# The first group's keys for four token tiles abreast, begun with half of w_ada's columns, with the first gate unit beside them

## The chip, the cores and the metric

The kernel runs on one core of one Trainium2 chip. The metric is device time in microseconds (us). Before the change the median of three runs is 1931.95 us (1931.21 to 1932.6). The engines are TensorE (PE; its weight loads are a row of their own, PEld), VectorE (DVE), ScalarE (ACT), GpSimd (POOL) and SyncE (SP), which issues every DMA here. Each engine takes its instructions strictly in the order in which they stand in its own program.

## The reference

One encoder layer is applied to two request groups (prompt and sample, each 1024 tokens by 1024 channels) with the same weights. A vector c per group gives shift, scale and gate; the input is RMS-normed and modulated; one wide projection feeds two attention branches and their gates:

```python
mod = jnp.einsum('bd,de->be', jax.nn.silu(c), w_ada) + b_ada
shift, scale, gate = jnp.split(mod, 3, axis=-1)
h = rms_norm(x, norm_g) * (1.0 + scale[:, None, :]) + shift[:, None, :]
proj = jnp.einsum('bsd,de->bse', h, w_in)
qa, ka, va, za, qb, kb, vb, zb, ga, gb = jnp.split(proj, [o1, o2, o3, o4, o5, o6, o7, o8, o9], axis=-1)
qa = rms_norm(qa.reshape(B, S, HQ_A, HEAD_DIM), qn_a)      # ka the same way, then both rotated
...
oa = gqa_attention(qa, ka, va) * jax.nn.silu(za)
ob = rms_norm(diff_attention(qb, kb, vb, lam), subln_g) * (1.0 - lam_init) * jax.nn.silu(zb)
merged = jax.nn.sigmoid(ga) * (oa @ w_proj_a) + jax.nn.sigmoid(gb) * (ob @ w_proj_b)
out = x + gate * (merged @ w_out)
```

(The last four lines are shortened here; the shapes are left out.)

## The kernel before

All matmuls of the projection work on pairs: a float32 operand is split into a rounded part ("hi", made by ACT with a Copy) and the rest ("lo", a subtraction), and a product is three matmuls, hi*hi, hi*lo and lo*hi. Weights are split by `split_w` (L192 on ACT, L194 on DVE or POOL), the modulated input h by `modulated`.

**The start of the first group** is `start`. SP issues, in order, two tiles of w_ada (1 MB each), small vectors, the first half of the transposed input (tokens 0 to 511, 2 MB), the other six tiles of w_ada that give shift and scale, the weights of keys and values (`C_KA`, 256 columns, 1 MB), and the other half of the input. w_ada comes in eight tiles: numbers 0 and 1 give the shift of channels 0 to 511, 2 and 3 their scale, 4 and 5 the shift of channels 512 to 1023, 6 and 7 their scale. For each pair, `ada` makes eight thin matmuls (L324), then `ada_end` copies the row (L342 on DVE), lays it as columns (L336, four matmuls of two columns) and adds the bias (L348, L352), which fills `modc`. Meanwhile ACT squares the input, DVE adds the squares (L278 to L283), PE sums them over the partitions (L291), POOL takes the power -1/2 (L301) and `spread` (L308) lays the result over the partitions. `x` is then multiplied by it (L394, six on DVE and two on POOL), scaled and shifted (L358 on ACT, L360 on DVE), and split (L363 on ACT, L364 on DVE). All this is done for eight chunks of 128 channels.

**The head of the first group** is `head`. Two streams are woven on PE: keys and values (`kva_gen`) for eight token tiles and then the first half of the queries (`qa_gen`), through `proj_tt` (L539: per token tile 8 chunks x 3 matmuls of 128x256), and the gate units (`z_gen`, L709: each unit 8 x 3 matmuls of 128x512). After each token tile `front` normalises and rotates on DVE (lines 554 to 582, with one power on POOL, L560), and `back` transposes on PE (L593) and splits (L595 on ACT, L596 on DVE); `LAG = 2` lets a token tile's `back` come two tiles later. Between the first two tiles and the rest, `start_late` normalises and modulates tokens 512 to 1023 (L412, L415 to L417). Then attention begins: scores (L743, L744), the maximum (L745, DVE), the exponential (L746, ACT), while further gate units and queries fill PE.

**The rest**: attention of branch A and B with the remaining projections woven in, the branch projections, the output projection; `ht_gen` prepares the second group's h beside the first group's output projection; then the second group goes through the same stages.

**What sets the order.** The kernel writes its instructions in the order of these generators; a scheduler then sets each engine's order from a model of its own, within the data dependences, the number of buffers in each pool, and the extra edges that `behind` adds. PSUM has two 1024-wide tiles `s`, three 512-wide `f` and one `a`. `gbank` takes an `s` tile for two of every five requests while attention is not running (`alone`).

## Time and profile before

| | us |
|---|---|
| median of three runs (range) | 1931.95 (1931.21 to 1932.6) |
| the profiled execution, its own time | 1934.43 |
| its span in the profile | 1932.7 |
| busy: PE, PEld, DVE, ACT, POOL | 1863.8, 1562.7, 1161.5, 760.0, 674.2 |
| mean granted TensorE clock | 0.985 |

The span begins with the first instruction, and the profiled execution lasts 1.7 us longer than it. In the rows of a timeline stand the start in us, the length from the first start to the last end, the engine, the line, the operation, the tiles (result<-operands, buffer numbers left out), the shape and the count; in brackets the engine's idle time ahead of it and what ended it. A row of a table by stretches gives, for each engine, the busy us and the number of instructions, then the granted clock (PEclk, 1.00 is full), the share of DMA time and GB/s. Matmuls overlap in the pipeline, so the rate is read from starts: two rows that begin 24 matmuls apart.

### The profile page before, as it was taken

The numbers are of one execution on the slowest core, as the hardware profiler recorded it, in microseconds if no ns is written. First come the engines' busy times: TensorE is split into PE (matmuls) and PEld (weight loads), VectorE is DVE, ScalarE is ACT, GpSimd is POOL, SyncE is SP. The second block draws the span as 40 slices with busy tenths as digits, with TensorE's granted clock in tenths as the row PEclk, the third lists the DMA queues.
The fourth block names the chain that finished last, engine by engine and source line by source line (L and its number), as shares of the span: only waits on it lengthen the run. The fifth ranks groups of instructions, "written<-read, shape, count | busy, mean of one in ns | idle before, by whom it ended". The sixth has DMA issues, their size and how long they took to land. (4 is left out here: it accounts for less than half of the span.)

```text
span 1932.7 us, 29441 instructions
## 1 busy us (share of the span) xinstructions
PE 1863.8 (96%) x10434; PEld 1562.7 (81%) x10434; DVE 1161.5 (60%) x1709; ACT 760.0 (39%) x1548; POOL 674.2 (35%) x912
## 2 busy tenths in 40 slices
PE   6989999999999998999999999999999899999999
PEld 3778878888888996788888777888888798877887
DVE  5787663444667366757467777445357736666731
ACT  4444442444445344323233455234445524442210
POOL 2233421433456254121222434024456616322110
PEclk8999999999999999999999999999999999999999
DMA  8136674546243355875631567564525423587531
GB/s 316 54 87 172 182 200 133 156 128 201 81 137 100 98 169 156 268 259 179 209 104 50 166 183 198 157 180 132 163 78 143 111 79 90 157 251 248 170 103 55
DMA packets 268883, 295.03 MB, mean 153 GB/s; under 512 B 35136, under 2 KB 217536, under 8 KB 268736
## 3 DMA queue, kind: packets, MB, share of 16 engines
q1 hardware_dynamic: 268736, 293.15, 51.0%
q8 instruction: 83, 1.36, 0.3%
q14 instruction: 64, 0.52, 0.1%
HBM read 133.59 MB, written 42.01 MB: 91 GB/s over the span
## 5 line engine op out<-in xcount | busy, mean ns | idle before, releaser
L709 PE MATMUL f<-u,w 128*128 128x512 f32 x2256 | 588.4, 398 | 1.3 <-ACT w L192 0.9
L539 PE MATMUL f<-w,u 128*128 128x256 f32 x3456 | 484.0, 286 | 1.9 <-DVE ev L719 0.9
L709 PEld LDWEIGHTS f<-u,w 128*128 128x128 f32 x2256 | 415.2, 190 | 85.2 <-issue 2.7
L539 PEld LDWEIGHTS f<-w,u 128*128 128x128 f32 x3456 | 456.8, 192 | 24.2 <-issue 2.7
L745 DVE TENSOR_REDUCE m<-s 128x1 f32<-128x1024 f32 x256 | 309.9, 1218 | 208.3 <-PE s L744 205.9
L746 ACT ACTIVATE p<-s,m 128x1024 f32<-128x1024 f32 x256 | 285.2, 1115 | 287.4 <-DVE m L745 219.2
L194 POOL TENSOR_TENSOR w<-st,w 128x512 fp32r<-128x512 f32 x168 | 223.0, 1345 | 455.9 <-ACT w L192 415.4
L787 DVE STREAM_TRANSPOSE p<-p 128x1024 f32<-128x1024 f32 x192 | 237.0, 1240 | 69.0 <-ACT p L746 59.3
L560 POOL TENSOR_TENSOR rs<-ss,nhalf 128x4 f32<-128x4 f32 (+1 forms) x112 | 109.1, 975 | 361.7 <-DVE ss L559 317.8
L744 PE MATMUL s<-u,sw 128*128 128x512 f32 x512 | 204.8, 400 | 0.0
L192 ACT ACTIVATE w<-st 128x512 fp32r<-128x512 f32 x196 | 115.1, 626 | 147.1 <-DMA st<-in_w_in_dram 92.2
L946 PE MATMUL f<-u,w 128*128 128x512 f32 x552 | 137.4, 398 | 3.9 <-DVE u L957 3.2
L819 PE MATMUL a<-q,u 128*128 128x256 f32 x512 | 132.8, 394 | 8.0 <-DMA q<-p 5.5
L946 PEld LDWEIGHTS f<-u,w 128*128 128x128 f32 x552 | 103.7, 190 | 27.4 <-DVE u L957 4.8
L819 PEld LDWEIGHTS a<-q,u 128*128 128x128 f32 x512 | 98.6, 198 | 24.9 <-issue 5.9
L802 PE MATMUL a<-q,u 128*64 128x256 f32 x1024 | 117.6, 382 | 1.0 <-DMA q<-p 1.0
L743 PE MATMUL s<-u 128*128 128x512 f32 x256 | 108.0, 422 | 10.2 <-ACT p L746 8.9
L596 DVE TENSOR_TENSOR u<-f,u 64x256 fp32r<-64x256 f32 (+1 forms) x196 | 80.6, 411 | 58.1 <-ACT u L595 53.1
L743 PE MATMUL s<-u,u 128*128 128x512 f32 x256 | 104.9, 410 | 8.4 <-DVE ev L719 4.3
L744 PEld LDWEIGHTS s<-u,sw 128*128 128x128 f32 x512 | 97.4, 190 | 17.5 <-issue 0.8
L977 PE MATMUL f<-u,w 128*128 128x512 f32 x456 | 105.6, 389 | 0.0
L786 DVE SCALAR_TENSOR_TENSOR p<-p,r,p 128x1024 f32<-128x1024 f32 x64 | 87.2, 1362 | 28.8 <-POOL r L772 24.2
(168 smaller groups left out, 1939.7 us busy)
## 6 DMA issues: line engine op xcount, KB each, us to landing
q<-p SPq DMA_DIRECT2D x768, 128.0 KB, 2.6
st<-in_w_in_dram SPq DMA_DIRECT2D x132, 256.0 KB, 3.1
zd<-ev SPq DMA_DIRECT2D x96, 256.0 KB, 2.6
sw<-u SPq DMA_DIRECT2D x256, 64.0 KB, 2.0
p<-zd SPq DMA_DIRECT2D x64, 256.0 KB, 4.1
u<-in_w_ada_dram SPq DMA_DIRECT2D x8, 1024.0 KB, 11.4
od<-oo SPq DMA_DIRECT2D x64, 128.0 KB, 2.4
st<-in_w_in_dram SPq DMA_DIRECT2D x64, 128.0 KB, 2.8
```

The costliest lines, as they stand in the source:

```text
L192: nc.scalar.activation(wh, st, AF.Copy)
L194: e.tensor_tensor(out=wl, in0=st, in1=wh.bitcast(F32), op=ALU.subtract)
L539: ins = nc.tensor.matmul(ps, lt[c][:, sl], w[:, c, wi, :], start=(k == 0), stop=(k == 23))
L709: ins = nc.tensor.matmul(ps, w[:, c, wi, e * P : (e + 1) * P], rt[c], start=(k == 0), stop=(k == 23),)
L743: nc.tensor.matmul(s[:, sl], q, k[:, sl], start=True, stop=False)
L744: nc.tensor.matmul(s[:, sl], sw, k[:, sl], start=False, stop=True)
L745: nc.vector.tensor_reduce(out=m, in_=s, axis=AX.X, op=ALU.max, negate=True)
L746: nc.scalar.activation(pt.rearrange("p (j c a) -> p j c a", j=4, c=8), s.rearrange("p (c a j) -> p j c a", c=8, j=4), AF.Exp, bias=m, accu ...
L787: nc.vector.transpose(pt, pt)
L802: lambda k=k, m=m: nc.tensor.matmul(acc[(LO, HI)[m]], u["v"][:, k], pT[m][:, k], start=(k == 0), stop=(k == 7))
L819: nc.tensor.matmul(acc, u["v"][:, k], pT[:, k], start=(k == 0), stop=(k == 7))
L946: nc.tensor.matmul(ps, w[:, c, wi, d * P : (d + 1) * P], o[:, oi, :], start=(k == 0), stop=(k == 11))
```

## The change

1. **Transfers and columns.** SP now issues two tiles of w_ada, the first half of x, w_ada 2 and 3, then the first half (512 channels) of the weights of keys and values, w_ada 4 and 5, the first half of the first gate unit's weights (`C_ZA`), w_ada 6 and 7, the second half of the keys' weights, the second half of x, and the second half of the gate's weights; the tables of the rotation come behind all these.
2. **Keys abreast.** `abreast` works chunk by chunk on four token tiles at once, in four accumulators that lie in the two `s` tiles. Chunks 0 to 3 need only w_ada 0 to 3, and are issued before the matmuls of w_ada 6 and 7; chunks 4 to 7 follow. Two gate units of 24 matmuls (256 columns of the gate in two times 128, tokens 0 to 511) are begun with chunks 0 to 3 as well, in an `a` and an `f` tile, and finished later. Then the second four token tiles are done abreast, with the third gate unit between, and the fourth behind them.
3. **A shorter modulation.** `modulate` replaces `modulated`, the tail of `start_late` and the body of `ht_gen`: per chunk DVE multiplies by scale and 1/rms in one instruction, ACT adds the shift and rounds (hi), DVE makes lo from x, shift and hi. The separate multiplication by 1/rms (L394), and in `ht_gen` the addition on POOL, are gone.
4. **Smaller edits.** The lo part of weights is always made on POOL (before: on DVE for every other piece while `alone`). `ada_end` lays its columns in the accumulator itself. `gbank` takes `s` tiles only from the middle of the first head on. The key's transposes of the first group use the `a` tile until then. The exponential of lambda is put behind a later instruction of ACT.

Line numbers below are those of the changed kernel: L336 is `ada`, L348 the laying of columns, L385, L391 and L378 the three instructions of `modulate` (DVE, ACT, DVE), L408 `abreast`, L780 `z_part`, L655 and L659/L660 the keys' and queries' transposes and splits, L602 `proj_tt`.

```diff
--- before.py
+++ after.py
...
+    wide = [False]
 
     def gbank():
         turn[0] += 1
-        if alone[0] and turn[0] % 5 in (0, 2):
+        if wide[0] and alone[0] and turn[0] % 5 in (0, 2):
             return sbank()[:, :512]
...
-        e = nc.vector if alone[0] and q % 2 else nc.gpsimd
+        e = nc.gpsimd
...
+    def split_early(w, half, sts):
+        for i, st in enumerate(sts):
+            split_w(w, half * 2 + i, st)
...
+    def load_early(pieces):
+
+        room = halves2(ptile())
+        sts = [r.rearrange("p (c n) -> p c n", c=2) for r in room]
+        for st, srcs in zip(sts, pieces):
+            load_piece(st, srcs)
+        return sts
...
-        row = halves2(ptile())[0]
+        row = rtile()
         nc.vector.tensor_copy(row, acc)
-        ps = gbank()[:, :8].rearrange("p (c g) -> p c g", g=2)
+        ps = acc[:, :8].rearrange("p (c g) -> p c g", g=2)
...
-    def modulated(ht, hf, xT, cs):
...
+    def modulate(ht, hf, xs, rsb, g=0):
+
+        acts = []
+
+        def low(c, x):
+            hi, lo = (part[c] for part in ht[hf])
+            return nc.vector.scalar_tensor_tensor(
+                out=lo, in0=x, scalar=modc[:, 0, c, g : g + 1], in1=hi.bitcast(F32), op0=ALU.add, op1=ALU.subtract
+            )
+
+        prev, ins = None, None
+        for c, x in xs + [(None, None)]:
+            if x is not None:
+                new = nc.vector.scalar_tensor_tensor(
+                    out=x, in0=x, scalar=modc[:, 1, c, g : g + 1], in1=rsb, op0=ALU.mult, op1=ALU.mult
+                )
+                if ins is not None:
+                    behind(new, ins)
+                ins = new
+                acts.append(nc.scalar.activation(ht[hf][0][c], x, AF.Identity, bias=modc[:, 0, c, g : g + 1]))
+            if prev:
+                new = low(*prev)
+                behind(new, ins)
+                ins = new
+            prev = c, x
+        return ins, acts
...
+    def four():
+        return [s[:, n * 512 : n * 512 + 256] for s in (sbank(), sbank()) for n in range(2)]
...
+    def abreast(ht, w, hf, ps, cs):
+
+        for c in cs:
+            for i in range(4):
+                sl = slice(i * P, (i + 1) * P)
+                for n, (part, wi) in enumerate(((0, 0), (0, 1), (1, 0))):
+                    latest[0] = nc.tensor.matmul(
+                        ps[i], ht[hf][part][c][:, sl], w[:, c, wi, :],
+                        start=(c == n == 0), stop=(c == NCH - 1 and n == 2),
+                    )
...
+    def start(ht, kva, zs):
+        front, back = kva
         nc.scalar.activation(cT[:, : NCH * 2], cT[:, : NCH * 2], AF.Silu)
         wts = [load_ada(n) for n in range(2)]
         dma(bcol, t["b_col"])
         dma(gcol, t["g_col"])
         nc.vector.tensor_scalar(out=bcol[:, 1, :], in0=bcol[:, 1, :], scalar1=1.0, scalar2=None, op0=ALU.add)
         xT = [load_xT0(0)]
-        wts += [load_ada(n) for n in range(2, 5)]
-        wts += [load_ada(n) for n in range(5, 8)]
-        kva_w.append(load_w(w_cols(w_in, (C_KA, 256)), early=True))
-        xT.append(load_xT0(1))
-        for n in range(8):
+        wts += [load_ada(n) for n in range(2, 4)]
+        cols = [w_cols(w_in, (c, 256)) for c in (C_KA, C_ZA)]
+        ws = [wpool.tile([P, NCH, 2, 256], F32R, tag="w", name=nm("w")) for _ in range(2)]
+        sts = []
+        for half in range(2):
+            for pieces in cols:
+                if len(sts) == 3:
+                    xT.append(load_xT0(1))
+                sts.append(load_early([pieces(half * 2 + i) for i in range(2)]))
+                if not half:
+                    for _ in range(2):
+                        wts.append(load_ada(len(wts)))
+        w, zw = ws
+        load_tables()
+        load_tables_A(states[0])
+        for n in range(4):
             ada(n, wts[n])
-            if n == 3:
-                rsb = spread(inv_rms(added(squares(xT[0]))))
-                for c in range(NCH):
-                    e = nc.gpsimd if c % 3 == 2 else nc.vector
-                    e.tensor_tensor(out=xT[0][c], in0=xT[0][c], in1=rsb, op=ALU.mult)
-            if n in (2, 4, 6, 7):
-                ada_end(n if n == 7 else n - 1)
-            if n == 4:
-                add_h(ht, 0, 0)
-                modulated(ht, 0, xT[0], range(4))
-        split_early(kva_w[0])
-        add_h(ht, 0, 1)
-        end = modulated(ht, 0, xT[0], range(4, 8))
-        sq = squares(xT[1])
-        return lambda: start_late(ht, xT, inv_rms(added(sq, end), latest[0]))
-
-    def start_late(ht, xT, rs):
-        rsb = spread(rs)
-        for c in range(NCH):
-            x = xT[1][c]
-            if c % 4 == 0:
-                add_h(ht, 1, c // 4)
-            nc.vector.scalar_tensor_tensor(
-                out=x, in0=x, scalar=modc[:, 1, c, 0:1], in1=rsb, op0=ALU.mult, op1=ALU.mult
-            )
-            nc.scalar.activation(x, x, AF.Identity, bias=modc[:, 0, c, 0:1])
-            nc.scalar.activation(ht[1][0][c], x, AF.Copy)
-            nc.vector.tensor_tensor(out=ht[1][1][c], in0=x, in1=ht[1][0][c].bitcast(F32), op=ALU.subtract)
+            if n == 1:
+                ada_end(1)
+        rsb = spread(inv_rms(added(squares(xT[0]))))
+        split_early(w, 0, sts[0])
+        ada_end(3)
+        add_h(ht, 0)
+        ps = four()
+        modulate(ht, 0, list(enumerate(xT[0]))[:4], rsb)
+        abreast(ht, w, 0, ps, range(4))
+        for n in range(4, 6):
+            ada(n, wts[n])
+        ada_end(5)
+        split_early(zw, 0, sts[1])
+        for n in range(6, 8):
+            ada(n, wts[n])
+        ada_end(7)
+        zps = [ps_a.tile([P, 512], F32, tag="a", name=nm("a")), fbank()]
+        first_w.append((zw, list(zps)))
+        drain(z_part(ht[0], zw, zps, 0, range(4)), z_part(ht[0], zw, zps, 1, range(4)))
+        split_early(w, 1, sts[2])
+        split_early(zw, 1, sts[3])
+        add_h(ht, 0)
+        end, acts = modulate(ht, 0, list(enumerate(xT[0]))[4:], rsb)
+        sums = added(squares(xT[1], acts), end)
+        abreast(ht, w, 0, ps, range(4, 8))
+        drain(islice(zs, 3))
+        rs = inv_rms(sums, latest[0])
+        bar[0] = placed[0]
+        drain(islice(zs, 2))
+        rsb = spread(rs, latest[0], halves2(ptile())[0])
+        bar[0] = placed[0]
+        drain(islice(zs, 1))
+        ks = [front(tt, ps[tt]) for tt in range(3)]
+        for _ in range(2):
+            add_h(ht, 1)
+        modulate(ht, 1, list(enumerate(xT[1])), rsb)
+        for tt in range(4):
+            back(tt, ks[tt])
+            if tt == 0:
+                ks.append(front(3, ps[3]))
+        ps = four()
+        abreast(ht, w, 1, ps, range(NCH))
+        drain(islice(zs, 3))
+        wide[0] = True
+        ks = [front(4 + i, ps[i]) for i in range(3)]
+        drain(islice(zs, 3))
+        back(4, ks[0])
+        ks.append(front(7, ps[3]))
+        back(5, ks[1])
+        return [(back, 4 + i, ks[i], True) for i in (2, 3)]
...
-        nc.scalar.activation(lam2, lam2, AF.Exp)
+        behind(nc.scalar.activation(lam2, lam2, AF.Exp), turned[0])
...
-            nc.gpsimd.tensor_scalar(
-                out=xt, in0=xt, scalar1=modc[:, 0, c, g : g + 1], scalar2=1.0, op0=ALU.add, op1=ALU.mult
-            )
-            for hf in range(2):
-                xh = xt[:, hf * 512 : (hf + 1) * 512]
-                nc.scalar.activation(ht[hf][0][c], xh, AF.Copy)
-                nc.vector.tensor_tensor(out=ht[hf][1][c], in0=xh, in1=ht[hf][0][c].bitcast(F32), op=ALU.subtract)
+                modulate(ht, hf, [(c, xt[:, hf * 512 : (hf + 1) * 512])], rsb[hf], g)
...
+        bank = gbank() if wide[0] else ps_a.tile([P, 512], F32, tag="a", name=nm("a"))
...
+    def z_part(ht, w, ps, e, cs):
+        hh, hl = ht
+        k = 3 * cs[0]
+        for c in cs:
+            if c and c in (*CUTS, cs[0]):
+                yield 1
+            for wi, rt in ((0, hh), (0, hl), (1, hh)):
+                ins = nc.tensor.matmul(
+                    ps[e], w[:, c, wi, e * P : (e + 1) * P], rt[c], start=(k == 0), stop=(k == 23),
+                )
+                if bar[0] is not None:
+                    behind(ins, bar[0])
+                    bar[0] = None
+                latest[0] = ins
+                k += 1
+
...
+        w, begun = first_w.pop() if first_w else (load_w(w_cols(w_in, (col, 256))), None)
...
+                done = begun and not hf
+                pss = begun if done else {e: gbank()}
+                yield from z_part(ht[hf], w, pss, e, range(4 if done else 0, NCH))
+                ps = pss[e]
...
+            qa = qa_gen(st, 0, start(st["ht"], kva_parts(st), zs))
+            weave((qa, 27, 0.0), (islice(zs, nz - 12), nz - 12, Z_HEAD_A[g]))
...
```

How the order moves, at three places on which the prediction rests. First PE from the third tile of w_ada to the first projection, before (tiles: `u` is a tile of w_ada or of h, `f` and `s` are accumulators, `w` weights):

```order
L324 MATMUL s_207<-u_173,cT 32x512 x4
L291 MATMUL f_238<-ones_c,q_224 128x1 x4
L324 MATMUL s_207<-u_175,cT 32x512 x4
L308 MATMUL s_248<-ident,rs_244 128x128 x4
L324 MATMUL f_263<-u_177,cT 32x512 x4
L336 MATMUL s_270<-pick,p_268 128x2 x4
L324 MATMUL f_263<-u_179,cT 32x512 x4
L324 MATMUL f_295<-u_181,cT 32x512 x4
L336 MATMUL f_302<-pick,p_300 128x2 x4
L324 MATMUL f_295<-u_183,cT 32x512 x4
L336 MATMUL s_314<-pick,p_312 128x2 x4
L539 MATMUL f_362<-w_185,u_277 128x256 x2
```

And in the changed kernel:

```order
L336 MATMUL f_230<-u_175,cT 32x512 x4
L298 MATMUL f_253<-ones_c,q_239 128x1 x4
L336 MATMUL f_230<-u_177,cT 32x512 x4
L316 MATMUL f_263<-ident,rs_259 128x128 x4
L348 MATMUL f_230<-pick,row_274 128x2 x4
L336 MATMUL f_346<-u_184,cT 32x512 x4
L336 MATMUL f_346<-u_186,cT 32x512 x4
L408 MATMUL s_284<-w_179,u_282 128x256 x2
L408 MATMUL s_285<-w_179,u_282 128x256 x2
L408 MATMUL s_284<-w_179,u_283 128x256
L408 MATMUL s_284<-w_179,u_282 128x256 x2
```

The first key matmuls now stand behind the matmuls of six tiles of w_ada instead of eight, and from the third tile on behind one laying of columns (L348) instead of three (L336).

Second, PE of the changed kernel where chunks 4 to 7 begin (`a_383` and `f_384` are the two gate units, `u_282`/`u_283` hi and lo of chunks 0 to 3, `u_417`/`u_418` of chunks 4 to 7):

```order
L780 MATMUL f_384<-u_282,w_180 128x512 x2
L780 MATMUL f_384<-u_283,w_180 128x512
L780 MATMUL f_384<-u_282,w_180 128x512 x2
L780 MATMUL f_384<-u_283,w_180 128x512
L780 MATMUL f_384<-u_282,w_180 128x512
L348 MATMUL f_366<-pick,row_375 128x2 x4
L408 MATMUL s_284<-w_179,u_417 128x256 x2
L408 MATMUL s_285<-w_179,u_417 128x256 x2
L780 MATMUL a_383<-u_417,w_180 128x512
L408 MATMUL s_284<-w_179,u_418 128x256
```

The laying of the scale of channels 512 to 1023 (L348 with `row_375`) stands behind the last gate matmul of chunks 0 to 3, and the first matmul that needs chunk 4 stands right behind it; before, no projection matmul stood between the layings.

Third, POOL where attention begins; before (`rs` is the power for a token tile's queries, `w` the lo part of weights):

```order
L560 TENSOR_TENSOR rs_1237<-ss_1236,nhalf 128x4
L194 TENSOR_TENSOR w_1410<-st_1411,w_1410 128x2x256
L194 TENSOR_TENSOR w_1410<-st_1415,w_1410 128x2x256
L194 TENSOR_TENSOR w_1410<-st_1419,w_1410 128x2x256
L560 TENSOR_TENSOR rs_1295<-ss_1294,nhalf 128x4
L194 TENSOR_TENSOR w_1410<-st_1423,w_1410 128x2x256
L560 TENSOR_TENSOR rs_1469<-ss_1468,nhalf 128x4
```

And in the changed kernel:

```order
L621 TENSOR_TENSOR rs_1258<-ss_1257,nhalf 128x4
L195 TENSOR_TENSOR w_1384<-st_1385,w_1384 128x2x256
L195 TENSOR_TENSOR w_1384<-st_1389,w_1384 128x2x256
L195 TENSOR_TENSOR w_1384<-st_1393,w_1384 128x2x256
L621 TENSOR_TENSOR rs_1305<-ss_1304,nhalf 128x4
L195 TENSOR_TENSOR w_1384<-st_1397,w_1384 128x2x256
```

In both, three pieces of the next weights stand ahead of the last token tile's power (`rs_1295` before, `rs_1305` now).

158 lines of the change are left out of this document (62 added, 96 removed).

## The prediction

> **What bounds the kernel now.** I read the page's busy shares first, then busy time by stretches of 25 us, then TensorE's timeline in the first 145 us, and last the other engines there.
>
> ```profile
> PE 1863.8 (96%) x10434; PEld 1562.7 (81%) x10434; DVE 1161.5 (60%) x1709; ACT 760.0 (39%) x1548; POOL 674.2 (35%) x912
> ```
>
> TensorE is busy in 1863.8 of 1932.7 us, so a change can win only from the 68.9 us in which it is idle, and from time at a lowered clock.
>
> ```profile
> 0.00:25.00 25.00, 13.94 (x67) 6.19 (x67) 7.92 (x18) 6.69 (x11) 2.93 (x9) 1.00 0.97 362
> 25.00:50.00 25.00, 17.94 (x100) 13.34 (x100) 20.60 (x31) 16.18 (x33) 7.53 (x6) 0.73 0.78 252
> 50.00:75.00 25.00, 22.07 (x120) 19.32 (x120) 18.86 (x52) 13.75 (x28) 5.46 (x7) 0.86 0.17 56
> 75.00:100.00 25.00, 23.38 (x166) 21.38 (x166) 17.97 (x63) 10.55 (x38) 6.76 (x7) 1.00 0.20 64
> 100.00:125.00 25.00, 23.88 (x177) 22.45 (x176) 22.11 (x59) 9.72 (x26) 8.46 (x8) 1.00 0.19 55
> 125.00:150.00 25.00, 20.39 (x88) 16.08 (x87) 20.23 (x30) 11.06 (x22) 6.91 (x6) 0.86 0.50 138
> 150.00:175.00 25.00, 25.00 (x154) 20.66 (x152) 17.86 (x20) 11.04 (x22) 9.36 (x14) 1.00 0.63 169
> ```
>
> The first number behind the length is TensorE's busy time. The first six rows lack 28.4 us, two fifths of all its idle time, and three show a lowered clock; from 150 us on TensorE is full. This is the stretch that the change rewrites. In its first 25 us DMA runs at 0.97 of its time: there the transfers are the limit.
>
> ```profile
> 16.34 1.94 PE L324 MATMUL s<-u,cT 128*32 128x512 f32 x8 [2.35 <-DMA u<-in_w_ada_dram]
> 20.30 1.93 PE L324 MATMUL s<-u,cT 128*32 128x512 f32 x8
> 22.16 1.12 PE L308 MATMUL s<-ident,rs 128*128 128x128 f32 x4
> 24.23 1.05 PE L336 MATMUL s<-pick,p 128*128 128x2 f32 x8
> ...
> 26.60 1.06 PE L324 MATMUL f<-u,cT 128*32 128x512 f32 x8 [0.33 <-DMA u<-in_w_ada_dram]
> 30.53 1.86 PE L336 MATMUL f<-pick,p 128*128 128x2 f32 x8 [2.86 <-DVE p L342]
> ...
> 39.40 7.91 PE L539 MATMUL f<-w,u 128*128 128x256 f32 x48
> ...
> 53.90 0.95 PE L291 MATMUL s<-ones_c,q 128*128 128x1 f32 x8
> ...
> 58.38 1.11 PE L308 MATMUL f<-ident,rs 128*128 128x128 f32 x4 [0.33 <-POOL rs L301]
> ...
> 93.41 3.26 PE L539 MATMUL f<-w,u 128*128 128x256 f32 x26
> ...
> 117.16 3.04 PE L539 MATMUL f<-w,u 128*128 128x256 f32 x24
> ...
> 120.17 3.11 PE L539 MATMUL f<-w,u 128*128 128x256 f32 x24
> ...
> 124.59 5.75 PE L709 MATMUL s<-u,w 128*128 128x512 f32 x24
> ...
> 137.54 0.79 PE L743 MATMUL s<-u,u 128*128 128x512 f32 x1 [1.50 <-ACT p L746]
> ...
> 139.69 6.45 PE L709 MATMUL f<-u,w 128*128 128x512 f32 x21
> ```
>
> The first projection matmul starts at 39.40. The last query tile ends at 123.28 (120.17 + 3.11), and the sixth gate unit starts at 139.69, behind eight key tiles, eight query tiles, five gate units and twelve score matmuls. The changed order puts the same work ahead of its sixth gate unit, so I compare the kernels there. At full clock 24 matmuls of 128x256 take 2.9 us (117.16 to the next such row, less two transposes) or 0.12 each, and 24 of 128x512 take 5.6, or 0.23 each.
>
> ```profile
> 45.78 1.22 DVE L278 TENSOR_TENSOR q<-q,q 128x1024 f32<-128x1024 f32 x1
> 46.92 2.31 DVE L281 TENSOR_TENSOR q<-q,q 128x1024 f32<-128x1024 f32 x1
> 60.84 5.39 DVE L412 SCALAR_TENSOR_TENSOR u<-u,modc,ev 128x512 f32<-128x512 f32 x8 [2.79 <-ACT ev L310]
> 72.12 0.28 DVE L562 TENSOR_TENSOR row<-row,rs 128x128 f32<-128x128 f32 x1
> 132.58 1.48 DVE L562 TENSOR_TENSOR row<-row,rs 128x256 f32<-128x256 f32 x1 [1.19 <-POOL rs L560]
> 135.03 1.22 DVE L745 TENSOR_REDUCE m<-s 128x1 f32<-128x1024 f32 x1
> ```
> ```profile
> 34.14 2.17 ACT L192 ACTIVATE w<-p 128x512 fp32r<-128x512 f32 x4
> 55.99 0.60 ACT L717 ACTIVATE ev<-f 128x512 f32<-128x512 f32 x1 [1.20 <-PE f L709]
> 66.84 0.72 ACT L415 ACTIVATE u<-u,modc 128x512 f32<-128x512 f32 x1
> ```
> ```profile
> 126.48 2.73 POOL L194 TENSOR_TENSOR w<-st,w 128x512 fp32r<-128x512 f32 x2 [0.91 <-ACT w L192]
> 131.54 1.01 POOL L560 TENSOR_TENSOR rs<-ss,nhalf 128x4 f32<-128x4 f32 x1 [0.51 <-DVE ss L559]
> ```
>
> These give the prices: 0.67 us for a product on DVE (5.39 over 8), about 0.25 for a small one (0.28, overlapped), 0.72 for ACT's shift, 0.54 for a split's hi, 0.60 for a tanh, 1.37 for a lo on POOL, 1.0 for a power.
>
> **The change part by part.** Times are from the span's start.
>
> *Transfers.* TensorE waits for the third w_ada tile at 16.34 (5 MB into the queue) and for the seventh at 26.60 (9 MB): 2.57 us per MB. By the new list w_ada 5 is whole at 8.5 MB, so at 25.3; w_ada 7 at 11 MB, 31.8; the gate weights' last piece at 14 MB, 39.5.
>
> *First key matmul.* Nothing changes up to `spread`, which ends at 23.3. The scale's laying (1.05) ends at 24.3; the multiplication L394 no longer stands in its way. Two small DVE instructions, the product and ACT's shift take 0.4 + 0.7 + 0.7: hi of chunk 0 at 26.1. TensorE must first pass w_ada 4 and 5: 25.3 + 1.1 = 26.4, against 39.40.
>
> *Chunks 0 to 3.* 48 key matmuls 5.8, six gate matmuls 1.4 and a laying 1.05 end at 34.7. DVE's eight instructions (5.4) and a row copy keep just ahead. The matmuls of w_ada 6 and 7 (2 x 1.06) end at 36.8, their data being there at 31.8; 18 gate matmuls (4.1) and the last laying end at 42.0.
>
> *The seam to chunk 4.* The laying stands last, so nothing covers what follows: 0.3 + 0.7 + 0.7 = 1.7. A DVE instruction beside POOL's can take double (2.31 against 1.22 above, POOL making lo parts), and here POOL makes those of the gate. Bounds 1.7 to 4; I take 2.0, near the bare price: 44.0.
>
> ```profile
> 28.00:30.00 2.00, 0.00 (x0) 1.00 1.06 386
> 30.00:32.00 2.00, 1.47 (x7) 0.53 1.09 395
> 44.00:46.00 2.00, 2.00 (x19) 1.00 0.14 32
> 58.00:60.00 2.00, 1.67 (x9) 0.50 0.34 131
> 66.00:68.00 2.00, 2.00 (x16) 1.00 0.00 0
> ```
>
> *The clock.* After 2.86 us of idleness the granted clock falls to half at 30, and after 39.40 it needs until about 44 to come back. The seam's 2.0 us with a thin laying ahead are near that. Bounds 0 and 2 us (half of 4); I take 1. The Trainium skill (TensorE: Matmul & The Clock Gate, Part 1) has the clock fall after an idle window of about 3.4 us and return after as long a busy one. By that rule the seam would cost no clock, and the sum would be 1 us better. The row above fell with 2.86 us, so here the rule is too kind, or its free-running window makes both possible.
>
> *Chunks 4 to 7.* 5.8 + five gate matmuls 1.2 + 1 for the clock end at 52.0; DVE (eight instructions from 42.3) and ACT keep ahead. Six gate matmuls, then the thin sums: 54.4. From these to `spread` before took 3.5 us (53.90 + 0.95 to 58.38), with other DVE work between. The instructions alone are 1.5; I take 2.5 for 1.5 to 4. Six gate matmuls lie within it. `spread` ends at 58.0, the last six gate matmuls at 59.4. ACT's next in order is that unit's tanh, and then hi: 0.6 + 0.7. TensorE goes on at 60.8.
>
> *Tokens 512 to 1023.* DVE has 16 modulations (10.7), a gate product (0.7) and some 25 small instructions of four `front`s (6.3) in one queue: 17.7 from 58.6, with 1.2 for hand-overs (0 to 5) to 77.5. TensorE has 17.0 us of work (96 x 0.12 + 24 x 0.23) from 60.8, so both bind together; what needs the last lo ends at 79.8.
>
> *The fourth gate unit* takes an `s` tile, which ACT must first have read: three weight splits, a tanh and small ones stand ahead, 2.7 in all (0 to 3): 82.5. The unit ends at 88.0. Then eight query tiles and a gate unit, which before took 93.41 to 123.28: 29.9, and 0.3 for transposes. Here 118.2.
>
> *Into attention.* Before: 123.28 to 139.69 less one gate unit (5.7), 10.7 us. The chain is the same now: three lo parts on POOL, the last power, DVE's maximum behind it, the exponential, the third score pair. I take 10.7 again (8 to 14): 128.9.
>
> *The rest.* All lo parts on POOL while attention is not running cost two more of 1.37 per weight tile and free DVE of as many. `ht_gen` drops eight POOL additions. In the second group's head and the output projections TensorE is full or nearly so; I take 0 (-2 to +2).
>
> The sixth gate unit starts at 128.9 instead of 139.69: 10.8 us. The profiled execution (1934.4) would take 1923.6. It lies 2.5 above the median of 1931.95, and from that it is **1921 us**.
>
> **The rivals.** (1) *No seams.* All lower bounds hold (seam and clock 1.3, sums 1.0, hand-overs 1.2, the `s` tile 2.7): 6 us more, 1915. For it: each part waits for something small. Against: nothing lies behind these waits. (2) *DVE eats the gain.* In tokens 512 to 1023 half of the 17.7 us takes double, +9: 1930. For it: the row of 2.31. Against: POOL has only five powers there, and the splits come behind. (3) *The transfers do not land in the listed order*, because eight are under way at once: w_ada 5 comes with its neighbours (gate's half, w_ada 6; 1.5 MB, 3.9 us), and w_ada 7 with the rest 3.9 later. The early start is then worth 6 less: 1927. Against: the waits of before fit one rate. (4) *Slower: POOL becomes the bound.* Two more lo parts stand ahead of each power; if the power comes later than the 5.8 us (two token tiles) by which `LAG` hides it, TensorE waits up to 2.7 us for each of some eight weight tiles in the two heads: +22 less 10.8, 1943. For it: the wait of 1.19 in the row at 132.58. Against: POOL is at 3 to 9 of 25 us in the first six rows.
>
> **How the numbers follow.** Forecast 0.60 (own range 1917 to 1926), rivals 0.15, 0.12, 0.06, 0.07. Kept out of 1914 to 1929 are the lower part of the first rival, most of the second and the fourth: under 0.2. The measurement can tell 0.2% or 3.9 us from no change. Faster by more: forecast, first rival and most of the third, 0.81; within: 0.12; slower: 0.07.
>
> **What would show it.** The first L408 at 26 to 27 us (over 30: the transfers); an idle of 2 us ahead of the first L408 with `u` of chunk 4 near 44, released by ACT; the granted clock there; DVE over 0.9 busy from 59 to 78; an idle ahead of the fourth L780 unit; the first L602 near 88; the sixth gate unit near 129; TensorE full from 145 on and in the second group as before. It would be wrong if L655 waited for POOL's powers, or if a later stage lost what the head won.

## The result, and the profile after

The changed kernel takes 1945.36 us (median of four, 1943.47 to 1946.11), the kernel before beside it 1932.28 (1931.21 to 1933.39): 1.0066 times as long, interval 1.005 to 1.0082. It is slower, by about 13 us; 1921 was predicted. The profiled execution of the changed kernel is the fastest of its four (1943.47, span 1941.7), so the two traces differ by only 9.0 us, and the sums below are made against these 9.0.

TensorE's own work is what it was:

```profile
PE 1862.6 (96%) x10434; PEld 1563.0 (81%) x10434; DVE 1144.0 (59%) x1677; ACT 759.1 (39%) x1536; POOL 695.6 (36%) x932
```

The same stretches of 25 us as before (TensorE's busy time stands behind the length; the number before the last two is its granted clock):

```profile
0.00:25.00 25.00, 13.90 (x68) 6.69 (x68) 7.24 (x19) 7.95 (x13) 4.38 (x10) 1.00 0.97 360
25.00:50.00 25.00, 22.29 (x139) 17.22 (x132) 15.84 (x23) 13.35 (x22) 8.08 (x6) 0.89 0.88 292
50.00:75.00 25.00, 22.20 (x133) 19.41 (x132) 20.02 (x55) 9.61 (x25) 4.33 (x6) 0.91 0.08 27
75.00:100.00 25.00, 17.38 (x110) 15.28 (x108) 17.90 (x45) 11.61 (x35) 13.46 (x13) 0.98 0.31 95
100.00:125.00 25.00, 23.83 (x161) 22.81 (x162) 18.64 (x60) 7.53 (x22) 4.51 (x5) 0.88 0.11 33
125.00:150.00 25.00, 16.23 (x80) 13.31 (x79) 21.39 (x39) 11.76 (x26) 8.36 (x7) 0.73 0.29 76
150.00:175.00 25.00, 25.00 (x156) 20.94 (x155) 17.45 (x23) 10.09 (x19) 4.74 (x8) 1.00 0.64 170
```

The row from 25 gains 4.4 us of busy time and a better clock. The rows from 75 and from 125 lose 6.0 and 4.2. TensorE's timeline names the places:

```profile
26.54 2.48 PE L408 MATMUL s<-w,u 128*128 128x256 f32 x16
...
45.21 1.22 PE L408 MATMUL s<-w,u 128*128 128x256 f32 x4 [2.39 <-ACT u L391]
...
62.80 0.50 PE L408 MATMUL s<-w,u 128*128 128x256 f32 x2 [1.30 <-ACT u L391]
...
84.88 5.74 PE L780 MATMUL s<-u,w 128*128 128x512 f32 x24 [1.51 <-ACT u L709]
...
90.59 3.13 PE L602 MATMUL f<-w,u 128*128 128x256 f32 x24
...
101.17 0.44 PE L655 MATMUL f<-ident,row 128*128 128x128 f32 x1 [7.27 <-DVE row L643]
101.27 5.09 PE L602 MATMUL f<-w,u 128*128 128x256 f32 x24
...
127.21 3.12 PE L602 MATMUL f<-w,u 128*128 128x256 f32 x24
...
137.64 0.66 PE L655 MATMUL s<-ident,row 128*128 128x128 f32 x2 [6.53 <-DVE row L643]
...
141.88 0.77 PE L824 MATMUL s<-u,u 128*128 128x512 f32 x1 [1.87 <-DVE u L660]
...
145.71 4.61 PE L780 MATMUL f<-u,w 128*128 128x512 f32 x17
```

The first keys start at 26.54, 13 us earlier than before. But TensorE waits 7.27 us for the rotated row of key tile 6, whose transposes stand right behind the first query tile, 6.53 us for that of query tile 6, where attention begins, and 1.87 behind that. After each long wait the clock is low: 24 query matmuls take 5.09 us instead of 3.1. The sixth gate unit begins at 145.71, against 139.69 before.

The rest can be read from the output projection, whose last matmul closes each group. In the line's answers (times in ns, then the first and last start in us), before:

```profile
L977 PE MATMUL f<-u,w x216: 389/389/389, 906.0 to 993.8; 128*128 128x512 f32 x108
...
L977 PE MATMUL f<-u,w x240: 388/389/389, 1841.5 to 1928.3; 128*128 128x512 f32 x120
```

and after:

```profile
L1058 PE MATMUL f<-u,w x216: 389/389/389, 910.4 to 998.1; 128*128 128x512 f32 x108
...
L1058 PE MATMUL f<-u,w x240: 388/389/389, 1850.5 to 1937.4; 128*128 128x512 f32 x120
```

The first group ends 4.3 us later (998.1 against 993.8). The second takes 939.3 us from there instead of 934.5, so 4.8 are lost in a part where the program does almost the same. The place is one wait near 1200, which the trace before does not have:

```profile
1204.95 0.79 PE L824 MATMUL s<-u,u 128*128 128x512 f32 x1 [5.60 <-ACT p L827]
```
```profile
1198.40 0.63 ACT L193 ACTIVATE w<-st 128x512 fp32r<-128x512 f32 x1 [2.03 <-DMA st<-in_w_in_dram]
1199.44 1.27 ACT L193 ACTIVATE w<-st 128x512 fp32r<-128x512 f32 x2 [0.41 <-DMA st<-in_w_in_dram]
...
1203.18 0.63 ACT L193 ACTIVATE w<-st 128x512 fp32r<-128x512 f32 x1 [1.92 <-DMA st<-in_w_in_dram]
1203.71 1.10 ACT L827 ACTIVATE p<-s,m 128x1024 f32<-128x1024 f32 x1
```
```profile
1184.46 8.52 SPq L877 DMA_DIRECT2D q<-p  x12
1193.08 0.55 SPq L803 DMA_DIRECT2D zd<-ev  x1
1193.72 1.50 SPq L214 DMA_DIRECT2D st<-in_w_in_dram  x3
```

Four weight splits stand ahead of the exponential on ACT, and ACT waits three times for their transfers. SP issued the first three of these transfers only behind twelve others, which took it 8.52 us; the fourth, which the exponential waits for last, it issued at 1200.40.

### The profile page after: what moved, and what is told of

Same layout as the page of the kernel before. It is cut to its first block, busy times and chain, and to the rows that moved or that the text cites. A ratio compares the mean times of both kernels' runs of the same rounds, so it can differ in the third digit from the quotient of the medians.

```text
span 1941.7 us, 29404 instructions
## 1 busy us (share of the span) xinstructions
PE 1862.6 (96%) x10434; PEld 1563.0 (81%) x10434; DVE 1144.0 (59%) x1677; ACT 759.1 (39%) x1536; POOL 695.6 (36%) x932
## 4 chain that ended last, share of the span: by engine, by line
PE 79%; DMA 6%; DVE 5%; POOL 3%; SPq 2%; issue 2%; ACT 1%; POOLq 0%; DVEq 0%; ACTq 0%
PE f L780 22%; PE f L602 18%; PE a L883 6%; PE f L1058 5%; PE s L824 5%; PE s L825 5%; PE f L1027 4%; PE s L1058 4%; PE a L900 3%; PE s L1027 3%; DMA row<-zd 2%; SPq L877 1%; POOL w L195 1%; PE s L408 1%; DMA st<-in_w_in_dram 1%
## 5 line engine op out<-in xcount | busy, mean ns | idle before, releaser
L780 PE MATMUL f<-u,w 128*128 128x512 f32 x2232 | 581.3, 397 | 0.0
L780 PEld LDWEIGHTS f<-u,w 128*128 128x128 f32 x2232 | 408.8, 189 | 82.1 <-issue 3.8
L602 PE MATMUL f<-w,u 128*128 128x256 f32 x3264 | 459.1, 286 | 1.1 <-DVE u L660 0.6
L602 PEld LDWEIGHTS f<-w,u 128*128 128x128 f32 x3264 | 432.4, 192 | 22.5 <-issue 2.7
L195 POOL TENSOR_TENSOR w<-st,w 128x512 fp32r<-128x512 f32 x192 | 253.0, 1336 | 474.3 <-ACT w L193 426.3
L1027 PE MATMUL f<-u,w 128*128 128x512 f32 x552 | 136.0, 395 | 4.6 <-DVE u L1038 3.2
L1027 PEld LDWEIGHTS f<-u,w 128*128 128x128 f32 x552 | 102.5, 188 | 27.9 <-DVE u L1038 5.1
L660 DVE TENSOR_TENSOR u<-f,u 64x256 fp32r<-64x256 f32 (+1 forms) x192 | 79.2, 413 | 58.7 <-ACT u L659 53.8
L1058 PE MATMUL f<-u,w 128*128 128x512 f32 x456 | 105.6, 389 | 0.0
L883 PEld LDWEIGHTS a<-q,u 128*64 128x64 f32 x1024 | 72.9, 137 | 39.6 <-issue 6.1
```

The source lines that it names most:

```text
L195: e.tensor_tensor(out=wl, in0=st, in1=wh.bitcast(F32), op=ALU.subtract)
L602: ins = nc.tensor.matmul(ps, lt[c][:, sl], w[:, c, wi, :], start=(k == 0), stop=(k == 23))
L780: ins = nc.tensor.matmul(ps[e], w[:, c, wi, e * P : (e + 1) * P], rt[c], start=(k == 0), stop=(k == 23),)
L883: lambda k=k, m=m: nc.tensor.matmul(acc[(LO, HI)[m]], u["v"][:, k], pT[m][:, k], start=(k == 0), stop=(k == 7))
L1027: nc.tensor.matmul(ps, w[:, c, wi, d * P : (d + 1) * P], o[:, oi, :], start=(k == 0), stop=(k == 11))
L1058: nc.tensor.matmul(ps, w[:, c, wi, e * P : (e + 1) * P], m[:, mi, :], start=(k == 0), stop=(k == 23))
```

## The experiments

Three reasons were open for the first group: the lo parts on POOL (theory A), the gate unit that no longer covers the start of attention (B), and key transposes that stand too early (C, E). TensorE work "covers" a wait when it stands in front of it and runs while other engines finish what TensorE needs next. For the second group the suspect was the order of its instructions (D). Each run has its ratio to the kernel before on the same chip. "Waits" are TensorE's idle times over 0.5 us between 86 and 150 us, added from the timeline (before 5.2, changed 15.7). "First" is the start of the first group's last output matmul, "second" the time from there to the last output matmul; both are from one profiled execution, so a difference of 2 us in them can be that execution's clock (last section).

| run | median, us | ratio (interval) | waits | first | second |
|---|---|---|---|---|---|
| before (its profile) | 1931.95 | | 5.2 | 993.8 | 934.5 |
| changed | 1945.36 | 1.0066 (1.005 to 1.0082) | 15.7 | 998.1 | 939.3 |
| changed, half of lo on DVE | 1943.72 | 1.0047 (1.0032 to 1.0063) | 14.2 | 993.7 | 943.9 |
| changed, all lo on DVE | 1946.25 | 1.0061 (1.0046 to 1.0076) | 15.1 | 998.3 | 942.2 |
| before, lo on POOL | 1945.85 | 1.0054 (1.0035 to 1.0072) | 8.7 | 997.8 | 942.2 |
| before, lo on POOL in first group | 1947.49 | 1.0067 (1.0052 to 1.0082) | 8.6 | 995.8 | 944.8 |
| changed, fourth gate unit woven in | 1947.85 | 1.0069 (1.0052 to 1.0086) | 16.9 | 999.4 | 944.1 |
| changed, fifth gate unit late | 1939.10 | 1.0029 (1.0014 to 1.0045) | 12.6 | 988.9 | 943.1 |
| changed, key transposes late | 1933.16 | 0.9995 (0.9985 to 1.0006) | 12.1 | 993.8 | 934.1 |
| these two and half of lo on DVE | 1938.98 | 1.0024 (1.0011 to 1.0036) | 10.7 | 991.5 | 941.7 |
| changed, second group's number | 1937.42 | 1.0009 (0.9997 to 1.0022) | 16.1 | 998.2 | 936.7 |
| key transposes late, fifth unit at -0.8 | 1936.11 | 1.0006 (0.9992 to 1.0019) | 12.9 | 994.6 | 934.3 |
| the same, half of lo on DVE | 1933.85 | 0.9992 (0.9978 to 1.0005) | 11.3 | 992.7 | 935.1 |
| fifth gate unit late, second group's number | 1931.02 | 0.9992 (0.9979 to 1.0004) | 10.8 | 989.9 | 936.6 |
| the same, half of lo on DVE | 1929.55 | 0.9979 (0.9967 to 0.999) | 11.0 | 987.6 | 933.7 |

### Who makes the lo parts

```diff
-        e = nc.gpsimd
+        e = nc.vector if alone[0] and q % 2 else nc.gpsimd
```

> The changed kernel with one edit undone: while attention is not running, every other lo part of the weights is made on DVE again. Theory A (the lo parts on POOL cause the new stalls): two of four lo parts (1.3 us each) leave the chain in front of key tile 6's power, so TensorE's wait of 7.27 us there falls to about 4.5; POOL's order where attention begins is unchanged, so the wait of 6.53 us there stays; with a similar gain in the second group about 1940 us. Theory B (the stalls come from the place of the key transposes and from the lack of a gate unit, whoever makes the lo parts): both waits stay within 1 us and the time is 1943 to 1947. A rival to both: DVE, with four lo parts more among the fronts, is later than before, the first wait grows to 9 and the time to 1948.

Key tile 6's wait fell to 5.78, that at attention's start stayed (6.52), and its interval overlaps that of the changed kernel. This is what theory B forecast, except that the edit took 1.5 us off the first wait, as theory A would have it in part. With all lo parts on DVE (`e = nc.vector if alone[0] else nc.gpsimd`):

> The changed kernel with all lo parts of the weights on DVE while attention is not running, none on POOL. In the changed kernel a DVE product of 128x128 that runs beside a lo part on POOL took 1.26 to 1.35 us instead of 0.29, about as long as the lo part. Theory A (it is this coincidence on POOL and DVE that makes key tile 6 late): the products take 0.29 throughout from 80 to 102, the four or five lo parts of 0.69 on DVE cost less than what they free, and the wait of 7.27 us falls to 3 or 4; with one chain of lo parts on POOL left where attention begins, 1939 to 1942. Theory E (the four fronts at once are too much work for the cover): DVE has 3 us of lo parts more, the wait stays between 5 and 8, and the time is 1942 to 1947.

In the changed kernel, DVE's products while POOL makes three lo parts (DVE first, then POOL):

```profile
83.45 1.35 DVE L623 TENSOR_TENSOR row<-row,rs 128x128 f32<-128x128 f32 x1 [0.88 <-POOL rs L621]
84.83 1.27 DVE L710 TENSOR_TENSOR row<-row,gka 128x128 f32<-128x128 f32 x1
86.14 1.26 DVE L634 TENSOR_TENSOR rc<-row,tab 128x128 f32<-128x128 f32 x1
...
91.58 0.29 DVE L710 TENSOR_TENSOR row<-row,gka 128x128 f32<-128x128 f32 x1
```
```profile
83.39 3.86 POOL L195 TENSOR_TENSOR w<-st,w 128x512 fp32r<-128x512 f32 x3
```

and with none on POOL there:

```profile
85.08 0.28 DVE L710 TENSOR_TENSOR row<-row,gka 128x128 f32<-128x128 f32 x1
86.42 0.29 DVE L634 TENSOR_TENSOR rc<-row,tab 128x128 f32<-128x128 f32 x1
...
100.70 0.45 PE L655 MATMUL f<-ident,row 128*128 128x128 f32 x1 [6.39 <-DVE row L643]
```

Both halves of theory A come apart. A product beside POOL does take as long as one lo part (1.29), and alone 0.29. But with that gone the wait is still 6.39: it is not what made key tile 6 late. The wait at attention's start (6.52 in this run) is not tested by it: there the lo parts stay on POOL in every run. In the kernel before, the edit alone:

> The kernel before with that one edit of the change alone: all lo parts of the weights on POOL. Theory A: lo parts ahead of powers are what costs, so this kernel is slower than before by 3 to 8 us, with waits of TensorE for the transposes in both heads. Theory B: in the old order a gate unit lies behind each such chain and the time stays within 2 us of 1932.

It costs 0.54%, more than theory A's 3 to 8 us and far from theory B's 2. But of the 11.7 us by which the second group's end lies later, 7.7 are in the second group, where the wait near 1200 stands too (6.67 us). So the next run separates the groups.

### The second group's order

```diff
+        second[0] = True        # in ht_gen
-        e = nc.vector if alone[0] and q % 2 else nc.gpsimd
+        e = nc.vector if alone[0] and q % 2 and second[0] else nc.gpsimd
```

> The kernel before with all lo parts on POOL in the first group alone; the second group is made as before, but the scheduler orders its first attention units anew, like in the changed kernel and in before with all lo parts on POOL. Theory D (the second group loses to that new order and to nothing that it does differently): from its first scores to its merge projection it takes 667 to 670 us instead of 661.5, with TensorE's wait of 4 to 6 us for an exponential near 1200; with the 3 us that the first group lost in before with all lo parts on POOL about 1941 us. Rival (the second group loses to its own lo parts on POOL, or to the shorter modulation): it takes 661 to 663 us as before, without that wait, and the time is about 1935.

```profile
1203.59 0.80 PE L745 MATMUL s<-u,u 128*128 128x512 f32 x1 [6.33 <-ACT p L748]
```

The kernel before, with nothing of its second group rewritten, has the wait and takes 944.8 us there instead of 934.5. That is theory D, with a larger loss than forecast: the stretch from the second group's first scores to its merge projection took 671.1 us instead of 667 to 670, and the time is 1947.49 instead of about 1941. The other way round, one number of the second group's weave in the changed kernel:

```diff
-    (1.229, 1.265, 0.9, 1.0, 0.85, 1.069),
+    (1.222, 1.265, 0.9, 1.0, 0.85, 1.069),
```

> The changed kernel with one number of the second group's first attention phase at 1.222 instead of 1.229. The program is the same on every engine up to the instructions in front of the stall near 1200 us, and the first group is the same throughout; only there the scheduler sets the four weight splits ahead of other exponentials. Theory D (the second group loses 6 to 7 us to the order that the scheduler happened on): the wait of 5.60 us for the exponential goes or falls below 2, the stretch from the second group's first scores to its merge projection falls from 667.8 to 661 to 664 us, and the time to 1938 to 1941. Rival (the weights' transfers are late whatever the order, so that a wait of this size comes back at another place of this phase): 666 to 669 us and 1943 to 1946.

There is no wait over 0.5 us from 1165 to 1225 now. On ACT the fourth split stands behind the exponential that it held up, with its data there:

```profile
1199.41 1.11 ACT L827 ACTIVATE p<-s,m 128x1024 f32<-128x1024 f32 x1
...
1200.50 0.63 ACT L193 ACTIVATE w<-st 128x512 fp32r<-128x512 f32 x1
...
1203.04 1.12 ACT L827 ACTIVATE p<-s,m 128x1024 f32<-128x1024 f32 x1 [1.38 <-DVE m L826]
```

From the second group's first scores to its merge projection it takes 663.1 us instead of 667.8, as expected; 2 us of this are given back behind it, so that the group falls from 939.3 to 936.7, and the first group is the same (998.1 and 998.2). So 4.7 us of this stretch, 2.6 of the group, are the order that the scheduler happened on. The ratio falls by more, from 1.0066 to 1.0009 or some 11 us; most of that is in no trace, since the spans of the two profiled executions differ by 2.5 us (1941.7 and 1939.2), and the two ratios come from separate measurements of four and of twelve executions. The wait near 1200, with 4.6 us or more, stands in every run whose second group takes 939 us or more, and in none of the others.

### What covers the two waits of the first group

Left to the weave, the fourth gate unit no longer stands ahead of the query tiles:

```diff
-        drain(islice(zs, 3))                        # ahead of back(4, ks[0])
-            weave((qa, 27, 0.0), (islice(zs, nz - 12), nz - 12, Z_HEAD_A[g]))
+            weave((qa, 27, 0.0), (islice(zs, nz - 9), nz - 9, Z_HEAD_A[g]))
```

> The changed kernel with the fourth gate unit no longer issued inside the start: it is left to the weave beside the query tiles, so the transposes of key tiles 4 to 7 spread over the query tiles and two gate units lie among them. Theory C (the wait of 7.27 us comes from the place of key tile 6's transposes, right behind the first query tile, with nothing behind them that could run): that wait falls below 2 us; the queries' weights are needed 5.7 us earlier, which may cost up to 3 us for their splits; the start of attention keeps its 6.5 us: about 1938 to 1941. Theory A (the chain through ACT, POOL and DVE is simply longer than the work at hand): the wait comes back at another transpose with 5 us or more, and the time stays at 1943 to 1947.

Waits of 5.95 and 4.36 us replace the one of 7.27, and 3.11 stay at attention's start, with 1947.85 us in all: theory C, that only the place was wrong, is refuted. The keys' rows are late wherever PE asks for them. Why key tile 6's row is late can be read on ACT. In the changed kernel:

```profile
79.57 2.52 PE L408 MATMUL s<-w,u 128*128 128x256 f32 x19
92.47 0.26 ACT L615 ACTIVATE row<-s 128x128 f32<-128x128 f32 x1
```

and in the run without the fourth gate unit there:

```profile
89.50 0.28 ACT L614 ACTIVATE row<-s 128x128 f32<-128x128 f32 x1 [0.84 <-PE s L654]
```

The matmuls of four key tiles end together at 82.1, but key tile 6 is copied out of its accumulator, which begins its front, only at 92.47. The kernel has three `row` tiles (`rtile`), and key tiles 3, 4 and 5 hold them until they are transposed; the transposes of 3 and 4 (90.56 and 90.45) stand behind the fourth gate unit in TensorE's order. In the run without that unit the trace names a transpose (L654) as what released the copy. From the copy to key tile 6's transposes it is 8.7 us (92.47 to 101.17), and TensorE has other work for the first 1.4 of them. With no lo part on POOL there the copy comes at 92.32, as late as in the changed kernel, which fits that faster products gained so little. No run gave the kernel a fourth `row` tile. The fifth gate unit behind the queries:

```diff
-Z_HEAD_A = (-0.35, -0.25)
+Z_HEAD_A = (-1.0, -0.25)
```

> The changed kernel with one number changed: the fifth gate unit, which was woven between the query tiles, stands behind them in the program, so that the order has its 24 matmuls between the last query tile and the first scores. Theory B (the 15.4 us from the last query tile to the sixth gate unit lack the gate unit that lay there before): the wait of 6.53 us for query tile 6's transposes falls below 2 us, the sixth gate unit begins about 4 to 6 us earlier, and the time is 1939 to 1941. Rival (the fronts of the queries are the bound in this stretch): without the gate unit between them the query tiles wait for their transposes instead, by about 5 us in all, and the time stays at 1943 to 1947.

```profile
82.63 5.78 PE L780 MATMUL s<-u,w 128*128 128x512 f32 x24 [1.51 <-ACT u L709]
...
98.85 0.45 PE L655 MATMUL f<-ident,row 128*128 128x128 f32 x1 [7.22 <-DVE row L643]
...
122.62 0.41 PE L655 MATMUL f<-ident,row 128*128 128x128 f32 x2 [2.26 <-DVE row L643]
...
128.60 0.41 PE L655 MATMUL f<-ident,row 128*128 128x128 f32 x2 [2.49 <-DVE row L643]
128.77 9.80 PE L780 MATMUL f<-u,w 128*128 128x512 f32 x42
```

Theory B had the time right: 6.53 and 1.87 are gone, and 42 gate matmuls run while the last rows are made. The rival's waits of about 5 us came as well: the queries now wait 0.65, 2.26 and 2.49. The first group ends 9.2 us earlier than in the changed kernel, 4.9 earlier than before; about 2.2 of it were there by the fourth gate unit already (82.63 against 84.88), where the program is still the same; that part is the clock of this execution and not the edit. The key transposes later:

```diff
-        back(5, ks[1])
-        return [(back, 4 + i, ks[i], True) for i in (2, 3)]
+        return [(back, 4 + i, ks[i], True) for i in (1, 2, 3)]
```

> The changed kernel with the transposes of key tiles 5, 6 and 7 put behind query tiles 1, 2 and 3 (in the changed kernel behind the fourth gate unit and query tiles 0 and 1). Theory E (four token tiles end at once, so the vector work of their four fronts, some 12 us, has only a gate unit and one query tile, 8.6 us, to hide behind): with two query tiles more ahead of key tile 6's transposes, 5.8 us, TensorE's wait of 7.27 us there falls below 2, while the start of attention keeps its wait of 6 to 7 us; about 1937 to 1940 us. Rival (the fronts of the query tiles queue behind those of the keys, so the wait only moves on): waits of 4 us or more in all come back between the query tiles and the time stays at 1942 to 1946.

```profile
96.53 4.72 PE L779 MATMUL s<-u,w 128*128 128x512 f32 x20
...
103.14 0.33 PE L654 MATMUL f<-ident,row 128*128 128x128 f32 x1 [1.06 <-DVE row L642]
...
128.99 0.42 PE L654 MATMUL f<-ident,row 128*128 128x128 f32 x2 [3.94 <-DVE row L642]
...
132.97 0.69 PE L654 MATMUL s<-ident,row 128*128 128x128 f32 x2 [3.56 <-DVE row L642]
```

The wait of 7.27 is 1.06. The time is better than theory E had it by luck: the second group's order fell well here (934.1). In front of key tile 6's transposes stand a second query tile and most of the fifth gate unit. Attention's start has none and waits 3.94 + 3.56 + 2.20.

Together these edits did not add up. First with `Z_HEAD_A` at -1.0 and half of the lo parts on DVE:

> The changed kernel with three edits at once: half of the lo parts on DVE while attention is not running, the transposes of key tiles 5 to 7 behind query tiles 1 to 3, and the fifth gate unit behind the queries. If the waits at key tile 6 and at attention's start are separate costs, the merge projection of the first group, which begins at 799.5 in before, 804.3 in the changed kernel and 795.8 with the gate unit alone moved, begins near 789 to 791; the second group keeps its loss of 6 to 7 us, so 1930 to 1934 in all. If they are one queue of vector work that only moves along, it begins near 796 again and the time is 1937 to 1940.

The merge projection begins at 796.8, near the 796 of one queue and not at 789 to 791, and the waits are 2.96, 5.28 and 2.41. Then with -0.8, which leaves the gate unit right behind the last query tile:

> The changed kernel with two edits: the transposes of key tiles 5 to 7 behind query tiles 1 to 3, and the number that sets the fifth gate unit's place at -0.8, which puts its 24 matmuls right behind the last query tile. The scheduler's second group is that of the run that had only the first edit and took 661.5 us there. If the two waits are separate costs, the first group's merge projection begins at 792 to 794 (799.8 with the first edit alone, 795.8 with a gate unit moved alone) and the time is 1925 to 1928, faster than before by 0.2 to 0.4%. If the fronts of the queries are one queue of vector work that the gate unit only postpones, it begins at 797 to 800 and the time is 1930 to 1933.

```profile
101.05 0.44 PE L654 MATMUL f<-ident,row 128*128 128x128 f32 x1 [4.44 <-DVE row L642]
...
129.36 0.44 PE L654 MATMUL s<-ident,row 128*128 128x128 f32 x2 [1.61 <-DVE row L642]
...
138.21 0.66 PE L654 MATMUL f<-ident,row 128*128 128x128 f32 x2 [6.82 <-DVE row L642]
```

A miss for both: the merge projection begins at 802.2 instead of 792 to 794 or 797 to 800. The gate unit that covered key tile 6 now stands behind the last query tile, so 4.44 us are back at key tile 6; and 6.82 come at the transposes of the last query tile. The one gate unit of cover is wanted at two places, and wherever it goes some 11 to 13 us of waits remain.

> The kernel of the run before in this list with half of the lo parts on DVE again while attention is not running. Theory A (a DVE product beside a lo part on POOL takes as long as that part): two lo parts fewer on POOL per weight tile, at 0.69 us each on DVE, let the keys' and queries' fronts end earlier by 1 to 3 us, and the time is 1 to 3 us below that run. Rival (vector work is the limit in the heads, and each lo part on DVE adds to it): 1 to 4 us above it.

It is 2.3 us faster, with overlapping intervals: not settled by this pair alone.

### Both causes mended

The fifth gate unit at -1.0 and 1.222 in the second group:

> The changed kernel with two numbers changed: the fifth gate unit behind the queries (as alone it gave 1939) and 1.222 in the second group's first attention phase (as alone it gave 1937). If the loss of the changed kernel is made of these two independent parts, the first group (up to its last output projection) ends near 989 as with the gate unit alone (993.8 before, 998.1 changed), and the second takes 935 to 938 from there, against 943 with the gate unit alone: 1928 to 1932, faster than before by up to 0.3%. Rival (the first group's gain is paid back where the order changes, as it was when the key transposes and the gate unit were moved together): 1934 to 1937.

The first group ends at 989.9, the second takes 936.6: they add, since they lie in different groups. Its fourth gate unit begins at 82.43 against 84.88, so 2.5 of the first group's 8.2 us are again the clock of one execution. At 0.9992 it is level with the kernel before.

> The kernel of the run before in this list with half of the lo parts on DVE while attention is not running. Theory A (what POOL's lo parts cost the products on DVE beside them): 1 to 3 us below that run. Rival (vector work is one queue in the head, whoever does the lo parts): within 1.5 us of it.

1.5 us less, again with overlapping intervals. The three pairs of runs that differ in this alone all go the same way (1.0066 and 1.0047, 1.0006 and 0.9992, 0.9992 and 0.9979), which speaks for half of the lo parts on DVE, though none settles it. This version, at 0.9979 (0.9967 to 0.999), is the only one measured faster than the kernel before, by 0.2%; as the best of fourteen kernels it would need a second measurement.

## Why the prediction was wrong

**What held.** The first key matmul: 26.4 predicted, 26.54 measured. The laying at the end of chunks 0 to 3: 42.0, 42.8. Resuming at chunk 4: 44.0, 45.21. Tokens 512 to 1023: 60.8, 62.80. The fourth gate unit: 82.5, 84.88, behind 1.51 us for its `s` tile; its end 88.0, 90.6. The 2.6 us of lateness are the clock (0.89 and 0.91 in the rows from 25 and 50) and a longer seam (2.39). The 48 key and five gate matmuls of chunks 4 to 7 took 9.8 us (45.21 to 55.01), where 7.0 and 1 for the clock were counted, so the clock's term was 2.8 in this execution, outside its bounds of 0 and 2; that the seam would cost no clock did not come. The last section has an execution where the clock from 50 to 75 was full.

**First failed step: "eight query tiles and a gate unit, which before took 93.41 to 123.28: 29.9, and 0.3".** They took 39.7 (90.59 to 127.21 + 3.12): 9.5 more, of which 7.27 is the wait for key tile 6 and most of the rest the cold clock behind it. The pace of before was that of keys whose tiles ended one after the other, each front beside the next tile's matmuls, so that three `row` tiles were enough. Abreast, four tiles end together at 82.1, but the fronts of key tiles 6 and 7 begin only at 92.47 and 93.10, when transposes behind the fourth gate unit have freed `row` tiles. The step left out this chain of 8.7 us from copy to transposes, with one query tile in front of its reader.

**Second failed step: "The chain is the same now ... I take 10.7 again".** It was 15.4 (130.33 to 145.71). The 10.7 came from subtracting a gate unit of 5.7 that stood inside the interval; but that unit was the cover of the chain. With the unit in it the stretch took 16.4 before, and it does not shrink by the unit's 5.7 when that work is done elsewhere. The run with the gate unit behind the queries bears this out: the waits of 6.53 and 1.87 are gone there. Without these two steps the sixth gate unit would have begun some 14 us earlier.

**Third failed step: "The rest ... I take 0 (-2 to +2)".** It is +3.0 in the profile: -1.7 in the rest of the first group, +4.8 in the second, of which two runs tie at least 2.6 to the scheduler's order. I had compared the order of instructions in the first 145 us only. The terms 2.6, 9.5, 4.7 and 3.0 make the 19.9 us between the 1923.6 forecast for the profiled execution and its 1943.47. The other 4.4 us between 1921 and 1945.36 come from the choice of execution: the profiled one lay 2.5 above its median before and lies 1.9 below it now.

**The rivals.** The slower case, POOL as the bound, had nearly the right time (1943) by luck: with no lo part on POOL while attention is not running the kernel is as slow (1.0061), and part of the loss is in the second group's order. "DVE eats the gain" looked at tokens 512 to 1023, where DVE's last modulation ended at 77.3 against 77.5 forecast; the loss came in the fronts behind them. The transfers landed in the listed order.

**What stays open.** That three `row` tiles make key tile 6 late is read from the traces; no run had a fourth. That the fronts' vector work is one queue that sets the end of the head is inferred from waits that move and do not add; no run took vector work away, and DVE is busy for only 17.9 of the 25 us from 75 to 100. How much of the 6.53 us at attention's start is POOL's is open too: three products of query tile 6's front took 1.49, 1.37 and 1.15 us there beside three lo parts, where others of their shape take 0.43.

## What to carry to other kernels

Before subtracting work from an interval, ask whether it covered a chain there; TensorE work that starts earlier is a gain only if the vector chain behind it also ends earlier. When tiles are made abreast, their followers come in one burst, so count that burst against the buffers that it needs and against the work that still stands in front of its reader. Where a scheduler sets the order, compare the order of the whole program: a change in the first tenth moved 5 to 10 us in the second half.

## What the runs showed of the hardware

A DVE product of 128x128 takes 0.29 us, but 1.26 to 1.35 beside a lo part on POOL, which itself takes 1.29: it takes about as long as a whole POOL instruction. The Trainium skill (SBUF — State Buffer, Summary: rules for kernel authors) says that a DVE instruction with two SBUF inputs and a GpSimd one that reads SBUF exclude each other: the later one fully blocks until the first is done. The runs agree, and add that removing the overlap gained only 0.9 us of a 7.27 us wait.

SP took 0.7 us for each issue of `q<-p` in the row at 1184.46 (8.52 over twelve), so a weight tile's transfers can be late by their place in SP's order alone.

The same instructions get different clocks in different executions. In the run with the fifth gate unit late, whose program is the same up to about 110 us:

```profile
0.00:25.00 25.00, 13.14 (x64) 6.43 (x68) 7.16 (x17) 7.95 (x13) 4.37 (x10) 0.80 0.97 360
...
50.00:75.00 25.00, 22.23 (x146) 19.50 (x146) 21.14 (x55) 10.25 (x25) 4.33 (x6) 1.00 0.08 28
```

Above these are 1.00 and 0.91; from 25 to 50 the two are alike (0.86 here, 0.89 above). Here the first key matmul starts at 28.36, 1.8 us later than above, and the fourth gate unit at 82.63, 2.2 us earlier. Such differences are as large as some of the edits' effects.
